# A shared ring of PSUM banks, wide feed-forward norms, and two moved steps in a two-layer fp32 trunk on one core

## The chip, the cores and the metric

The kernel runs on one core of one Trainium2 chip, as one launch. The metric is device time in microseconds (us). Five engines work side by side: PE (TensorE: matmuls and transposes), DVE (VectorE), ACT (ScalarE), POOL (GpSimd) and SP (SyncE, which here only issues transfers). PE writes its products to PSUM, which has eight banks of 128 partitions x 512 fp32 numbers.

## The reference

A trunk of two layers works on 512 tokens of width 1024, in fp32. A layer is: half a feed-forward block, a mixer, a cross-attention to 256 memory tokens, half a second feed-forward block. Every step normalises x and adds its result to x:

```python
for layer in range(2):
    x = x + 0.5 * swiglu(rmsnorm(x, ffn_pre_norm[layer]), w_gu, w_down)      # 1024 -> 2 x 2816 -> 1024
    h = rmsnorm(x, mix_norm[layer])
    x = x + (even_mixer(h) if layer == 0 else mla_mixer(h))
    x = x + memory_cross_attention(rmsnorm(x, ...), rmsnorm(mem, ...))       # 4 heads of 256
    x = x + 0.5 * swiglu(rmsnorm(x, ffn_post_norm[layer]), w_gu, w_down)
```

`rmsnorm(x, g)` is x * rsqrt(mean(x*x) + 1e-6) * g. The mixer of layer 1 (MLA) projects h to a query latent of 512, a key-value latent of 256 and 32 rotary columns, normalises both latents, expands them to 16 heads of 96 (queries and keys) and 64 (values), and does causal softmax attention.

## The kernel before

**Data.** x lies transposed, as eight tiles `x0` to `x7` of 128 features x 512 tokens. Each matmul operand is split into a high part and a low remainder (fp32r), and `mm3` makes one product of three matmuls: high x high, low x high, high x low. Weights come from memory in granules of up to 512 KB (`gran`): SP issues the transfer, ACT casts the high part (L112), POOL, in some places DVE, subtracts to get the low part (L117). The raw tiles have three buffers and the split ones four, so the splitting runs some groups ahead of the matmuls.

**Order.** The program is written for a scheduler that puts instructions on each engine's queue by its own estimate of when they can start; where two could, the earlier one in the program goes first. `with self.queued():` only orders: what is in it goes behind the last recorded matmul on PE. A tile with `bufs=n` gets one of n places as it comes free, and the wait for its last readers is put on the instruction that writes it.

**Norms.** The gain is folded into the operands (`prep`), and the factor 1/rms per token is applied afterwards. `squares` sums the squares of x over the eight tiles into `sqs` (128 x 512). `stats` then sums over the partitions with four one-column products (tokens onto partitions: L172, an fp32 product is two records in the profile), and `rsqrt` works on 128 x 4 numbers by a bit estimate and three Newton steps, 11 DVE instructions in all. In the feed-forward block the factors must stand along the free dimension: four DVE instructions put them on diagonals (`dg`), `spread` multiplies those by ones (L189, four products of 128 columns), and ACT copies the result to `rbc`. `stats` is queued behind group `s0` of the up projection and `spread` behind the next. A group is 24 matmuls of 512 columns. `gated` then multiplies each group by `rbc` on DVE and frees its bank. There are five `mm` banks, two `A` banks and one for the norms (`st`). `s0` is 0, but 3 in the first block, where the first two groups use the `A` banks.

**Launch.** SP issues the first weight granule in two parts (128 KB and 384 KB), then `x1` to `x7`; ACT issues the gains and `x0`. ACT casts part one, makes the high part of `x0` (L150), casts part two, makes the high part of `x1`, and so on. PE meanwhile runs 12 products of a tile of ones with itself (L75).

**MLA.** `mla_in` makes the query latent (`cq`), then the key-value latent token tile by token tile on four banks; after all four it runs `lora` for `cq` and for `ckv`: an `rsqrt`, a scaling on DVE (L642), transposes on PE into two `tp` banks (L646), a cast by ACT (L649) and a subtraction by DVE. In `mla_attn`, one turn of the loop does, in program order: the logits of head n on three `lg` banks (`scores`: matmuls, a maximum on DVE, the exponential on ACT, L871), the transposes of head n-1's exponentials (`weights`: three units on two `pt` banks, L885, copied out by ACT L890 or DVE L892), the transposes of queries and keys of head n+2 (`turn`: one `pt` bank each, L780, read by ACT and DVE), and some projections as filling. One `av` bank and two `A` banks make up the eight.

**Cross-attention.** `memkv` projects the memory in four chunks c of four granules q. After chunk 0 its own norm is finished. `fins` (transposes of a key head into `at`, two banks, L1074, read by ACT L1078 and DVE L1079) are queued behind granules (1, 3), (2, 1), (2, 3) and (3, 1). The `stats` of x for the queries is queued at the end of chunk 1 and uses an `at` bank too.

Of the kernel before, what the change touches and what calls it, by code (L numbers as in the profile page):

```python
# [14 lines left out]
P = 128  # L15
D = 1024
S = 512
KT = D // P
# [3 lines left out]
EPS = 1e-6  # L22
# [4 lines left out]
class Trunk:  # L27
# [32 lines left out]
    def constants(self):  # L60
        nc, cp, a = self.nc, self.cp, self.a
        self.gc = self.t(cp, [P, 10, KT], "gc")
        self.ones = self.t(cp, [P, P], "ones")
        nc.vector.memset(self.ones, 1.0)
        self.x = [self.t(self.xp, [P, S], f"x{f}") for f in range(KT)]

        nc.scalar.dma_start(out=self.gc, in_=a["gcols"])
        nc.scalar.dma_start(out=self.x[0], in_=a["xT"][0])
        self.first = self.first_gran(a["w_gu0"][0]) if self.stop in (None, 1) else None
        for f in range(1, KT):  # L70
            nc.sync.dma_start(out=self.x[f], in_=a["xT"][f])

        ps = self.psA()
        for _ in range(12):
            nc.tensor.matmul(ps[:, 0:P], lhsT=self.ones, rhs=self.ones, start=True, stop=True)  # L75
        self.ident = self.t(cp, [P, P], "ident")
        make_identity(nc, self.ident)
        self.rbc = self.t(cp, [P, S], "rbc")
# [11 lines left out]
    def first_gran(self, src):  # L90

        nc = self.nc
        raw = self.t(self.wr, [P, KT * P], "wr")
        hi = self.t(self.ws, [P, KT * P], "wh", F32R)
        lo = self.t(self.ws, [P, KT * P], "wl", F32R)
        parts = (slice(0, 2 * P), slice(2 * P, KT * P))
        for c in parts:
            nc.sync.dma_start(out=raw[:, c], in_=src[:, c])

        def split(i):  # L100
            self.split(hi[:, parts[i]], lo[:, parts[i]], raw[:, parts[i]])
        r = lambda z: z.rearrange("p (k c) -> p k c", k=KT)
        return r(hi), r(lo), split
# [22 lines left out]

    def rsqrt(self, ssq, n, scale, eps, shape=None):

        nc, sp = self.nc, self.sp
        v = self.t(sp, [P, n], "rs_v", bufs=3)  # L130
        nc.vector.tensor_scalar(out=v, in0=ssq, scalar1=scale, scalar2=eps, op0=ALU.mult, op1=ALU.add)
        y = self.t(sp, [P, n], "rs_y", bufs=3)
        nc.vector.tensor_scalar(out=y.bitcast(I32), in0=v.bitcast(I32), scalar1=-0.5, scalar2=float(0x5F3759DF),
                                op0=ALU.mult, op1=ALU.add)
        u = self.t(sp, [P, n], "rs_u", bufs=2)
        for _ in range(3):
            nc.vector.tensor_tensor(out=u, in0=y, in1=y, op=ALU.mult)
            nc.vector.scalar_tensor_tensor(out=u, in0=u, scalar=-0.5, in1=v, op0=ALU.mult, op1=ALU.mult)
            nc.vector.scalar_tensor_tensor(out=y, in0=u, scalar=1.5, in1=y, op0=ALU.add, op1=ALU.mult)
        return y  # L140

    def prep(self, g, f):

# [23 lines left out]
    def stats(self, pp, tag, bufs=None, bc=False):  # L167

        nc = self.nc
        ps = self.t(pp, [P, S], tag, bufs=bufs)  # L170
        for t in range(NT):
            nc.tensor.matmul(ps[:, t:t + 1], lhsT=self.sqs[:, t * P:(t + 1) * P], rhs=self.ones[:, 0:1],  # L172
                             start=(t == 0), stop=(t == NT - 1), skip_group_check=True)
        y = self.rsqrt(ps[:, 0:NT], NT, 1.0 / D, EPS)
        self.rc = self.t(self.sp, [P, NT], "rc", bufs=2)
        nc.vector.tensor_copy(out=self.rc, in_=y)
        if not bc:
            return
        self.dg = self.t(self.sp, [P, NT, P], "dg", bufs=1)
        for t in range(NT):  # L180
            nc.vector.tensor_scalar(out=self.dg[:, t, :], in0=self.ident, scalar1=self.rc[:, t:t + 1], scalar2=None,
                                    op0=ALU.mult)

    def spread(self, pp, tag, bufs=None):

# [45 lines left out]
    def ffn(self, w_gu, w_dn, g_next, out=None):  # L231
        nc, tc = self.nc, self.tc
        with tc.tile_pool(name=self.nm("ffn"), bufs=1) as fp, \
                tc.tile_pool(name=self.nm("ffps"), bufs=5, space=bass.MemoryType.PSUM) as pp:
            H = NFF // 2


            s0 = 3 if self.first else 0
            todo = []

            def gated(j, pg, pu):
                t1 = self.t(fp, [P, S], "t1", bufs=2)
                t2 = self.t(fp, [P, S], "t2", bufs=2)
                nc.vector.tensor_tensor(out=t1, in0=pg, in1=self.rbc, op=ALU.mult)  # L244
                nc.scalar.activation(out=t1, in_=t1, func=AF.Silu)
                nc.vector.tensor_tensor(out=t2, in0=pu, in1=self.rbc, op=ALU.mult)  # L246
                nc.vector.tensor_tensor(out=t2, in0=t2, in1=t1, op=ALU.mult)  # L247
                ah = self.t(fp, [P, S], f"ah{j}", F32R)
                al = self.t(fp, [P, S], f"al{j}", F32R)
                self.split(ah, al, t2, "act", "dve")  # L250
                return ah, al

            for half in range(2):
                acts = []
                for j in range(H):
                    jj = half * H + j

                    pg, pu = [self.psA() if self.first else self.t(pp, [P, S], "mm") for _ in range(2)]
                    for ps, w in ((pg, w_gu[jj]), (pu, w_gu[NFF + jj])):
                        wh, wl = self.first[:2] if self.first else self.gran(w, KT, P)  # L260
                        self.first = None
                        for k in range(KT):
                            self.mm3(ps, (wh[:, k, :], wl[:, k, :]), (self.hh[k], self.hl[k]), k == 0, k == KT - 1)
                        n = 2 * jj + (ps is pu)
                        if n in (s0, s0 + 1):
                            with self.queued():
                                self.stats(pp, "st", 1, True) if n == s0 else self.spread(pp, "st", 1)
                    todo.append((j, pg, pu))
                    if 2 * jj > s0 or s0 == 0:
                        for z in todo:  # L270
                            acts.append(gated(*z))
                        todo = []
                for m in range(KT):
                    ps = self.psA()
                    for k0, nk in ((0, 6), (6, 5)):
                        wh, wl = self.gran(w_dn[half * KT + m, :, k0 * P:(k0 + nk) * P], nk, P)
                        for k in range(nk):
                            self.mm3(ps, (wh[:, k, :], wl[:, k, :]), acts[k0 + k], k0 + k == 0, k0 + k == H - 1)
                    nc.vector.scalar_tensor_tensor(out=self.x[m], in0=ps, scalar=0.5, in1=self.x[m],  # L279
                                                   op0=ALU.mult, op1=ALU.add)  # L280
                    if half == 1:
                        if g_next is not None:
                            self.prep(g_next, m)
                            self.squares(m)
                        if out is not None:
                            nc.sync.dma_start(out=out[m], in_=self.x[m])
# [366 lines left out]
    def mla_in(self, p, pp, cT, krr, skr, lg, tk):  # L653
        nc, a = self.nc, self.a
        w = a["mla_w_inq"]
        cq = self.t(p, [P, NT, 512], "cq")
# [3 lines left out]
        s1 = self.t(p, [P, NT], "ls1")  # L660
        s2 = self.t(p, [P, NT], "ls2")
        ps = self.banks(pp, "mmmm")
# [6 lines left out]
        ps = self.banks(pp, "AAmm")  # L669
        kv = self.tok_rows(ps, [(a["mla_w_inkv"][:, k0 * 288:(k0 + nk) * 288], nk)  # L670
                                for k0, nk in ((0, 3), (3, 3), (6, 2))], 288, True)
        for t in kv:
# [2 lines left out]
            nc.scalar.activation(out=scr[:, 0:256], in_=ckv[:, t, :], func=AF.Square, accum_out=s2[:, t:t + 1])  # L675
            nc.scalar.activation(out=kr[:, t, :], in_=ps[t]()[:, 256:288], func=AF.Copy, scale=r)
            nc.scalar.activation(out=scr[:, 0:32], in_=kr[:, t, :], func=AF.Square, accum_out=skr[:, t:t + 1])
        self.lora(p, pp, cq, 512, s1, cT, lg, 0)
        self.lora(p, pp, ckv, 256, s2, cT, lg, 4)
        tm = self.t(p, [P, NT, 16], "krt")  # L680
        for o, (x, y, op) in enumerate((("c1", "s2", ALU.subtract), ("s1", "c2", ALU.add))):
# [5 lines left out]
    def mla_attn(self, p, pl, pp, cT, krr, skr, gqk, neg, tq, o):  # L687
# [86 lines left out]
        def turn(st, h):  # L774

            r = []
            for src, nm in ((st["qs"], "q"), (st["ks"], "k")):
                ps = self.t(pp, [P, S], "pt", bufs=2)
                for t in range(NT):
                    self.pe = nc.tensor.transpose(out=ps[0:96, t * P:(t + 1) * P], in_=src[:, t, h, :], identity=self.ident)  # L780
                hi = self.t(p, [96, S], f"{nm}Th", F32R, bufs=3)
# [59 lines left out]
        def scores(n, qk):  # L841
# [6 lines left out]
                self.sums = self.t(p, [P, 2, NT], "asm", bufs=2)  # L848
            sm = self.sums[:, n % 2]
            for u, blks in enumerate(((3,), (2, 0), (1,))):  # L850
                z = self.t(pp, [P, S], "lg", bufs=3)
                for x, i in enumerate(blks):
                    c0 = QA[i][1]
                    wd = (i + 1) * P
# [21 lines left out]
        def weights(pb, wT, units):  # L876

            for u in units:
                blks = ((0,), (1, 3), (2,))[u]
                ps = self.t(pp, [P, S], "pt", bufs=2)  # L880
                for j in blks:
                    c0 = KA[j][1]
                    for i in range(j, NT):
# [117 lines left out]
    def memkv(self, p, pp, l, kT, V, gqk):  # L1001
# [24 lines left out]
        for c in range(4):  # L1026
# [12 lines left out]
            if rm is None:  # L1039
# [4 lines left out]
                y = self.rsqrt(st[:, 0:MT], MT, 1.0 / D, EPS)  # L1044
                rm = self.t(p, [P, MT], "rm")
                nc.vector.tensor_copy(out=rm, in_=y)
            if c == 1:

                with self.queued():
                    self.stats(pp, "at", 2)  # L1050
# [208 lines left out]
```

## Time and profile before

| | |
|---|---|
| median of three runs | 2269.89 us (2269.11 to 2270.17) |
| the profiled execution | 2276.53 us |
| its span, first to last instruction | 2274.8 us |
| PE busy in the span | 2248.7 us (99%) |
| DVE, ACT, POOL busy | 893.8, 865.5, 1017.5 us |

The profile describes one execution. Its span is 1.7 us below that execution's own time, and that time is 6.6 us over the median of the runs. A line of the timeline reads: start, duration, engine, line of the kernel, operation, tile written and tiles read, shape, count, and in brackets how long the engine stood idle before it and which instruction ended that.

### The profile page before, as it was taken

What the parts mean: (1) busy time and instruction counts of PE and PEld (TensorE: products, weight loads), DVE (VectorE), ACT (ScalarE), POOL (GpSimd) and SP (SyncE); (2) the same over time, 40 slices, a digit from 0 to 9 for tenths busy, and PEclk for the clock granted to TensorE, in tenths of its full rate; (3) what the DMA queues carried; (4) which work ended last, traced back from release to release, by engine and by line L of the source; (5) the groups of instructions that cost most, each with busy time, mean ns of one, the idle gap of its engine ahead of it and who ended that gap; (6) DMA issues with size and microseconds to landing.
All of it is one profiled execution on the core that took longest, in us unless ns stands there. A gap on an engine that the chain in (4) does not pass through costs nothing. (4 is left out here: it accounts for less than half of the span.)

```text
span 2274.8 us, 27672 instructions
## 1 busy us (share of the span) xinstructions
PE 2248.7 (99%) x10496; PEld 1851.0 (81%) x10496; DVE 893.8 (39%) x1697; ACT 865.5 (38%) x1428; POOL 1017.5 (45%) x854
## 2 busy tenths in 40 slices
PE   9999999999999999999999999999999999999999
PEld 7888888777888888888888888887777788888887
DVE  5211223465745422123422022377667555221220
ACT  5222233456544322223322222356656443222221
POOL 5545546112143454555554555536321424545543
PEclk9999999999999999999999999999999999999999
DMA  5223323211432322332322332321113312323222
GB/s 167 87 85 116 93 84 130 84 54 54 139 107 66 93 93 84 111 93 82 113 93 83 113 96 85 99 86 56 38 37 122 121 56 93 93 83 113 93 83 94
DMA packets 67493, 208.60 MB, mean 92 GB/s; under 512 B 8608, under 2 KB 10784, under 8 KB 67360
## 3 DMA queue, kind: packets, MB, share of 16 engines
q1 hardware_dynamic: 67072, 206.52, 29.4%
q8 instruction: 83, 1.36, 0.2%
q14 instruction: 50, 0.41, 0.1%
q10 hardware_dynamic: 288, 0.30, 0.1%
HBM read 204.70 MB, written 2.10 MB: 91 GB/s over the span
## 5 line engine op out<-in xcount | busy, mean ns | idle before, releaser
L117 POOL TENSOR_TENSOR wl<-wr,wh 128x512 fp32r<-128x512 f32 (+2 forms) x752 | 941.7, 1273 | 1048.5 <-ACT wh L112 1048.1
L112 ACT CAST wh<-wr 128x1024 fp32r<-128x1024 f32 (+2 forms) x422 | 406.7, 964 | 1059.7 <-PE mm L124 573.5
L123 PE MATMUL mm<-hh,wh 128*128 128x512 f32 x1408 | 548.7, 390 | 0.0
L125 PE MATMUL mm<-hh,wl 128*128 128x512 f32 x1408 | 547.9, 389 | 0.0
L124 PE MATMUL mm<-hl,wh 128*128 128x512 f32 x1408 | 547.8, 389 | 0.0
L124 PEld LDWEIGHTS mm<-hl,wh 128*128 128x128 f32 x1408 | 264.3, 188 | 55.1
L123 PEld LDWEIGHTS mm<-hh,wh 128*128 128x128 f32 x1408 | 264.3, 188 | 54.8
L125 PEld LDWEIGHTS mm<-hh,wl 128*128 128x128 f32 x1408 | 264.3, 188 | 54.7
L123 PE MATMUL A<-ah,wh 128*128 128x512 f32 x704 | 277.4, 394 | 0.0
L125 PE MATMUL A<-ah,wl 128*128 128x512 f32 x704 | 276.0, 392 | 0.0
L124 PE MATMUL A<-al,wh 128*128 128x512 f32 x704 | 273.2, 388 | 0.0
L246 DVE TENSOR_TENSOR t<-mm,rbc 128x512 f32<-128x512 f32 x87 | 60.2, 692 | 389.3 <-PE mm L125 389.3
L279 DVE SCALAR_TENSOR_TENSOR x<-A,x 128x512 f32<-128x512 f32 x64 | 44.3, 692 | 357.7 <-PE A L125 357.7
L125 PEld LDWEIGHTS A<-ah,wl 128*128 128x128 f32 x704 | 132.1, 188 | 31.0
L124 PEld LDWEIGHTS A<-al,wh 128*128 128x128 f32 x704 | 132.1, 188 | 29.6
L123 PEld LDWEIGHTS A<-ah,wh 128*128 128x128 f32 x704 | 132.4, 188 | 26.4
L244 DVE TENSOR_TENSOR t<-mm,rbc 128x512 f32<-128x512 f32 x87 | 60.2, 692 | 190.6 <-PE mm L125 185.3
L88 DVE TENSOR_TENSOR al<-t,ah 128x512 fp32r<-128x512 f32 x88 | 84.3, 958 | 58.4 <-ACT ah L84 58.4
L123 PE MATMUL A<-hh,wh 128*128 128x512 f32 x256 | 103.8, 405 | 1.4 <-ACT hh L150 1.2
L124 PE MATMUL A<-hl,wh 128*128 128x512 f32 x256 | 101.2, 395 | 0.8 <-DVE hl L151 0.8
L125 PE MATMUL A<-hh,wl 128*128 128x512 f32 x256 | 101.1, 395 | 0.6 <-POOL wl L117 0.6
L84 ACT CAST ah<-t 128x512 fp32r<-128x512 f32 x88 | 54.6, 621 | 64.9 <-DVE t L247 64.7
(348 smaller groups left out, 2991.9 us busy)
## 6 DMA issues: line engine op xcount, KB each, us to landing
wr<-in_w_gu SPq DMA_DIRECT2D x175, 512.0 KB, 3.5
wr<-in_w_dn SPq DMA_DIRECT2D x64, 384.0 KB, 3.1
wr<-in_w_dn SPq DMA_DIRECT2D x64, 320.0 KB, 2.9
wr<-in_xmem_wkv SPq DMA_DIRECT2D x32, 512.0 KB, 3.7
wr<-in_xmem_wq SPq DMA_DIRECT2D x16, 512.0 KB, 3.5
wr<-in_xmem_wo SPq DMA_DIRECT2D x16, 512.0 KB, 3.6
wr<-in_sbg_w_zv SPq DMA_DIRECT2D x12, 512.0 KB, 3.6
wr<-in_sbg_w_qk SPq DMA_DIRECT2D x8, 512.0 KB, 3.6
```

What stands on the lines that cost most here:

```text
L84: nc.scalar.copy(out=hi, in_=src)
L88: e.tensor_tensor(out=lo, in0=src, in1=hi.bitcast(F32), op=ALU.subtract)
L112: nc.scalar.copy(out=hi, in_=raw)
L117: e.tensor_tensor(out=lo_[:, c], in0=raw[:, c], in1=hi[:, c].bitcast(F32), op=ALU.subtract)
L123: mm(out, lhsT=A[0], rhs=B[0], start=start, stop=False, skip_group_check=True)
L124: mm(out, lhsT=A[0], rhs=B[1], start=False, stop=False, skip_group_check=True)
L125: self.pe = mm(out, lhsT=A[1], rhs=B[0], start=False, stop=stop, skip_group_check=True)
L244: nc.vector.tensor_tensor(out=t1, in0=pg, in1=self.rbc, op=ALU.mult)
L246: nc.vector.tensor_tensor(out=t2, in0=pu, in1=self.rbc, op=ALU.mult)
L279: nc.vector.scalar_tensor_tensor(out=self.x[m], in0=ps, scalar=0.5, in1=self.x[m], op0=ALU.mult, op1=ALU.add)
```

## The change

1. **Launch.** SP issues the first part of the granule, `x0`, `x1`, the second part, then `x2` to `x7`; ACT issues only the gains. PE runs 7 products of ones, not 12.
2. **Feed-forward norms.** `stats_rows` replaces `stats` and `spread` in `ffn`: one product of ones (128 x 128) with `sqs` (128 x 512) puts every token's sum on all partitions, and the `rsqrt` runs on 128 x 512 numbers and ends in `rbc`. Its two helper tiles come from the pool of `sq`.
3. **Latents.** `lora` for `cq` stands behind token tile 1 of the key-value latent, no longer behind tile 3.
4. **Ring.** The three `lg` and two `pt` banks become five banks with one tag, `z`.
5. **Moved sums.** The `stats` of x in `memkv` moves from the end of chunk 1 to the end of chunk 2.

```diff
         nc.scalar.dma_start(out=self.gc, in_=a["gcols"])
-        nc.scalar.dma_start(out=self.x[0], in_=a["xT"][0])
         self.first = self.first_gran(a["w_gu0"][0]) if self.stop in (None, 1) else None
-        for f in range(1, KT):
+        for f in range(2 if self.first else 0, KT):
             nc.sync.dma_start(out=self.x[f], in_=a["xT"][f])
-        for _ in range(12):
+        for _ in range(7):
             nc.tensor.matmul(ps[:, 0:P], lhsT=self.ones, rhs=self.ones, start=True, stop=True)
...
-        for c in parts:
-            nc.sync.dma_start(out=raw[:, c], in_=src[:, c])
+        nc.sync.dma_start(out=raw[:, parts[0]], in_=src[:, parts[0]])
+        for f in range(2):
+            nc.sync.dma_start(out=self.x[f], in_=self.a["xT"][f])
+        nc.sync.dma_start(out=raw[:, parts[1]], in_=src[:, parts[1]])
...
+    def stats_rows(self, pp, tag, bufs=None):
+        nc = self.nc
+        ps = self.t(pp, [P, S], tag, bufs=bufs)
+        self.pe = nc.tensor.matmul(ps, lhsT=self.ones, rhs=self.sqs, start=True, stop=True)
+        v = self.t(self.sp, [P, S], "sq", bufs=2)
+        u = self.t(self.sp, [P, S], "sq", bufs=2)
+        self.rsqrt_into(self.rbc, v, u, ps, 1.0 / D, EPS)
...
-                        if n in (s0, s0 + 1):
+                        if n == s0:
                             with self.queued():
-                                self.stats(pp, "st", 1, True) if n == s0 else self.spread(pp, "st", 1)
+                                self.stats_rows(pp, "st", 1)
...
-        self.lora(p, pp, cq, 512, s1, cT, lg, 0)
+            if t == 1:
+                with self.queued():
+                    self.lora(p, pp, cq, 512, s1, cT, lg, 0)
         self.lora(p, pp, ckv, 256, s2, cT, lg, 4)
...
-                ps = self.t(pp, [P, S], "pt", bufs=2)
+                ps = self.t(pp, [P, S], "z", bufs=5)
                 for t in range(NT):
...
-                z = self.t(pp, [P, S], "lg", bufs=3)
+                z = self.t(pp, [P, S], "z", bufs=5)
                 for x, i in enumerate(blks):
...
-                ps = self.t(pp, [P, S], "pt", bufs=2)
+                ps = self.t(pp, [P, S], "z", bufs=5)
                 for j in blks:
...
-            if c == 1:
+            if c == 2:
                 with self.queued():
                     self.stats(pp, "at", 2)
```

`rsqrt_into` is the old body of `rsqrt` with the tiles handed in; the places that call `rsqrt` do as before.

## Rows read from the trace of the kernel before

**Rows 1.** The head of the profile page: the span, then each engine's busy us, its share and its instructions.

```profile
span 2274.8 us, 27672 instructions
PE 2248.7 (99%) x10496; PEld 1851.0 (81%) x10496; DVE 893.8 (39%) x1697; ACT 865.5 (38%) x1428; POOL 1017.5 (45%) x854
```

**Rows 2.** The waits of PE over the whole span: what waited, for what, us in total, times, longest.

```profile
PE pt L780 <- DVE wT L892: 4.2, 6, 1.4
PE A L123 <- ACT sq L758: 2.5, 1, 2.5
PE at L172 <- DVE kl L1079: 2.1, 2, 1.7
...
PE A L123 <- ACT ch L649: 1.4, 1, 1.4
...
PE pt L780 <- DVE qTl L88: 1.2, 1, 1.2
PE pt L780 <- DVE sqr L736: 1.1, 1, 1.1
PE pt L780 <- ACT wT L890: 1.0, 4, 0.3
```

**Rows 3.** [...]

```profile
1612.60:1615.80 3.20, 3.20 (x12) 3.20 (x11) 1.29 (x2) 0.68 (x1) 3.20 (x7) 0.50 0.00 0
1766.20:1769.40 3.20, 3.20 (x9) 2.51 (x8) 3.20 (x20) 1.04 (x1) 0.00 (x0) 0.50 0.19 28
1769.80:1773.00 3.20, 3.20 (x17) 2.64 (x16) 1.30 (x3) 1.78 (x3) 0.00 (x0) 1.00 0.72 245
...
1.10:4.80 3.70, 3.68 (x17) 3.68 (x18) 0.43 (x1) 1.69 (x2) 0.28 (x1) 1.00 0.75 198
```

**Rows 4.** The timeline of the launch, PE, ACT and DVE.

```profile
1.12 4.70 PE L75 MATMUL A<-ones 128*128 128x128 f32 x24 [1.12 <-DVE ones L64]
...
6.23 0.72 ACT L150 ACTIVATE hh<-x,gc 128x512 fp32r<-128x512 f32 x1 [2.29 <-DMA x<-in_xT]
...
7.00 0.50 PE L123 MATMUL A<-hh,wh 128*128 128x512 f32 x1 [1.18 <-ACT hh L150]
...
8.58 4.72 DVE L151 SCALAR_TENSOR_TENSOR hl<-x,gc,hh 128x512 fp32r<-128x512 f32 x7
...
15.90 0.50 PE L125 MATMUL A<-hh,wl 128*128 128x512 f32 x1 [0.63 <-POOL wl L117]
```

**Rows 5.** Transfers: issuing queue, count, KB of one, us from issue to landing.

```profile
x<-in_xT ACTq DMA_DIRECT2D x1, 256.0 KB, 4.9
...
wr<-in_w_gu SPq DMA_DIRECT2D x1, 128.0 KB, 2.7
```

**Rows 6.** The timeline at the start of layer 0's second feed-forward block, PE, DVE and POOL.

```profile
765.36 0.95 PE L172 MATMUL st<-ones,sqs 128*128 128x1 f32 x8
766.17 0.49 PE L123 MATMUL mm<-hh,wh 128*128 128x512 f32 x1
...
771.76 1.05 PE L189 MATMUL st<-dg,ones 128*128 128x128 f32 x8
772.56 0.48 PE L123 MATMUL mm<-hh,wh 128*128 128x512 f32 x1
...
762.82 1.77 DVE L165 TENSOR_TENSOR sqs<-sqs,sq 128x512 f32<-128x512 f32 x1
...
775.41 0.69 DVE L247 TENSOR_TENSOR t<-t,t 128x512 f32<-128x512 f32 x1 [0.66 <-ACT t L245]
...
772.89 2.55 POOL L117 TENSOR_TENSOR wl<-wr,wh 128x512 fp32r<-128x512 f32 x2 [3.84 <-ACT wh L112]
```

**Rows 7.** The timeline of the MLA latents, PE, ACT and DVE.

```profile
1519.73 1.04 PE L646 MATMUL tp<-ident,cq 128*128 128x128 f32 x8
1522.13 0.45 PE L123 MATMUL A<-wh,ch 128*128 128x384 f32 x1 [1.36 <-ACT ch L649]
...
1521.39 0.69 ACT L649 ACTIVATE ch<-tp,lorag 128x512 fp32r<-128x512 f32 x1
...
1518.27 1.68 DVE L642 TENSOR_SCALAR cq<-cq,rs_y 128x512 f32<-128x512 f32 x4
```

**Rows 8.** The timeline of one turn of the attention loop (logits of head 5), PE, ACT and DVE.

```profile
1610.15 0.64 PE L780 MATMUL pt<-ident,qs 128*96 128x128 f32 x4 [0.90 <-DVE wT L892]
1612.14 0.77 PE L780 MATMUL pt<-ident,ks 128*96 128x128 f32 x4 [1.35 <-DVE wT L892]
...
1609.57 0.36 ACT L871 ACTIVATE pb<-lg,anm 128x128 f32<-128x128 f32 x1
...
1609.91 0.47 ACT L871 ACTIVATE pb<-lg,anm 128x256 f32<-128x256 f32 x1
...
1611.67 0.41 DVE L892 COPY wT<-pt 128x256 f32<-128x256 f32 x1
```

**Rows 9.** The timeline of layer 1's memory projection, PE and DVE.

```profile
1764.02 1.05 PE L172 MATMUL at<-ones,sqs 128*128 128x1 f32 x8 [1.74 <-DVE kl L1079]
...
1763.48 0.48 DVE L1079 SCALAR_TENSOR_TENSOR kl<-at,gqk,kh 128x256 fp32r<-128x256 f32 x1
...
1777.02 0.60 PE L1074 MATMUL at<-ident,tk 128*128 128x128 f32 x4
...
1778.12 0.88 DVE L1079 SCALAR_TENSOR_TENSOR kl<-at,gqk,kh 128x256 fp32r<-128x256 f32 x2
```

More of the change, by code (lines that the diff above doesn't have):

```diff
@@ L127, in rsqrt, with rsqrt_into @@
     def rsqrt(self, ssq, n, scale, eps, shape=None):
-        nc, sp = self.nc, self.sp
+        sp = self.sp
         v = self.t(sp, [P, n], "rs_v", bufs=3)
+        y = self.t(sp, [P, n], "rs_y", bufs=3)
+        u = self.t(sp, [P, n], "rs_u", bufs=2)
+        self.rsqrt_into(y, v, u, ssq, scale, eps)
+        return y
+    def rsqrt_into(self, y, v, u, ssq, scale, eps):
+        nc = self.nc
         nc.vector.tensor_scalar(out=v, in0=ssq, scalar1=scale, scalar2=eps, op0=ALU.mult, op1=ALU.add)
-        y = self.t(sp, [P, n], "rs_y", bufs=3)
         nc.vector.tensor_scalar(out=y.bitcast(I32), in0=v.bitcast(I32), scalar1=-0.5, scalar2=float(0x5F3759DF),
                                 op0=ALU.mult, op1=ALU.add)
-        u = self.t(sp, [P, n], "rs_u", bufs=2)
         for _ in range(3):
@@ L139, in rsqrt @@
             nc.vector.scalar_tensor_tensor(out=y, in0=u, scalar=1.5, in1=y, op0=ALU.add, op1=ALU.mult)
-        return y
     def prep(self, g, f):
@@ L182, in stats @@
                                     op0=ALU.mult)
+    def stats_rows(self, pp, tag, bufs=None):
+        nc = self.nc
+        ps = self.t(pp, [P, S], tag, bufs=bufs)
[3 more added lines that the diff above has]
+        self.rsqrt_into(self.rbc, v, u, ps, 1.0 / D, EPS)
     def spread(self, pp, tag, bufs=None):
```

## The prediction

> **What bounds the kernel now.** The head of the page comes first: PE is busy 2248.7 of 2274.8 us [rows 1], the other engines under half. PE is the bound, and a change can help in three ways only: PE does less work, PE stands still less (26.1 us in all), or PE runs less of its work at the low clock. Second, PE's list of waits [rows 2], which names the places. A few lines carry it: the attention of layer 1 waits 7.5 us in the four lines on `pt` (4.2 + 1.2 + 1.1 + 1.0), the memory projection 2.1 us in its `stats`, the latents 1.4 us on a cast. The 2.5 us on L758 is an activation's square, which this change does not touch. Third, the granted clock by stretches [rows 3]: in two of those shown, right behind long waits, the clock is at 0.50. In the one at 1766 PE has 9 matmuls in 3.2 us, in the next 17. Last, the timelines of the five edited places [rows 4 to 9].
>
> **Feed-forward norms, four blocks.** The removed pieces are seen start to start: the one-column products take PE from 765.36 to 766.17, 0.81 us, the spreading from 771.76 to 772.56, 0.80 us [rows 6]. The new product passes the same 512 columns through the same kind of fp32 product as the spreading did, so I take its 0.80 us. The 0.81 us goes. One change between kinds of product goes too; it has no row of its own and can't cost more than the 0.49 us of the record behind it, of which I put in a tenth. Taken 0.85 a block, **3.4 us**; bounds 2.8 (the wide product is 0.15 slower) to 4.0.
>
> On DVE the eleven instructions of the chain go from 128 x 4 to 128 x 512 numbers. The nearest rows of that size are 0.69 us for a product of two tiles and 1.77 us for a sum of two tiles that ran beside POOL [rows 6], so the chain takes 7.6 to 19.5 us. It is costed at nothing, because the banks cover it. Sums end at 766.2, so `rbc` is there between 773.8 and 785.7. Group 0's bank is next wanted by group 5. A group takes 5.6 us (766.17 to 771.76), groups 2 to 4 begin about 772, so group 5 begins about 788.5. Even the slow chain and one multiplication, 786.4, comes before. In the first block the sums stand behind group 3 and group 7 wants group 2's bank, again three groups or 16.8 us later, but two groups are multiplied first: at 19.5 + 2 us that is 4.7 us late, once. POOL works 2.55 of 5.6 us, so I expect some 10 us and nothing lost. Behind the chain on DVE stand only the gate's own instructions. ACT loses its copy.
>
> POOL, in turn, may be held up by the chain. Its split at 772.89 goes into the buffer that the group just ended has freed, so it is wanted four groups later, about 789. It ends at 775.4; even 7.6 us more leaves 5 us. [...]
>
> **Ring, 16 heads.** A turn of the loop asks for banks in the order logits L0 L1 L2, transposes P0 P1 P2, query Q, key K. Before, the last five share two banks, so K waits until DVE has copied P2, and Q until P0 or P1 is copied. With five in a ring, P2 takes L0's bank, Q that of L1, K that of L2, each freed by an exponential. In the turn shown [rows 8], K starts at 1612.14, behind a copy begun at 1611.67. L2's exponential is over at 1610.38. L1's is over at 1609.93, so Q gains little (1610.15 to about 1610.0), and K can follow at 1610.4 to 1610.6. Of 2.25 us of waiting some 1.6 go, 70%. Of 7.5 us that is 5.3; I take **5.0 us**, with bounds 3.0 (only K gains) and 9.5 (all, with 0.15 us of refilling saved at each of 13 waits). The ring adds a wait too: the next L1 and L2 must wait for the copies of P1 and P2, and all of PE is queued behind. But a filling of twelve matmuls comes first, over 2 us, and the last copy ends 0.06 us before K's start even now.
>
> The low clock at 1612.6 [rows 3] follows 2.25 us of waiting with four transposes between. PE's work in it would take half: 1.6 us. If the waits shrink to 0.7 us I expect no drop; taken **1.2 us**, bounds 0 and 1.6.
>
> **Moved sums, two layers.** The 2.1 us [rows 2] arise because an `at` bank comes free only when DVE, busy with two chains, has made the key's low part at 1763.48 [rows 9]. At the new place the transposes run at 1777.02 and both low parts are made from 1778.12 to 1779.00, so the sums meet a free bank after about 1.6 us, which the matmuls put between fill or nearly fill. Taken **1.9 us**, bounds 1.2 and 2.4 (with refilling). The result is first wanted after chunk 3, 48 matmuls or 11 us later (a group's 24 take 5.6 us, 0.233 each): its 4-column chain is hidden. The low clock at 1766.2 goes with the 1.74 us wait: 8 of 17 matmuls are missing from 3.2 us, 1.5 us; taken **1.2 us**, bounds 0 and 1.5.
>
> **Latents.** The scaling ends at 1519.95, the transposes start at 1519.73, and ACT casts only at 1521.39, after other work; PE waits 1.36 us [rows 7]. Ahead of tile 3's work ACT could cast at about 1520.6, which is 0.8 us. Against it: if the transposes are queued among tile 3's matmuls, PE stands at them until the scaling is done, and 24 matmuls stand behind. Those matmuls then cover the cast, so the loss is at most about 1.5 us. Taken **0.5 us**, bounds -1.5 and 1.4.
>
> **Launch.** ACT's first use of `x0` is at 6.23, PE's first matmul at 7.00 [rows 4]; the transfer took 4.9 us, the 128 KB before it 2.7 us [rows 5]. Directly behind those, 256 KB at the 198 GB/s of this stretch [rows 3] is 1.3 us: `x0` lands near 4.8, 1.3 us earlier. SP issues one transfer more ahead of `x2`, ACT one fewer; bytes ahead of `x2` are the same, and from there DVE's 0.67 us a tile (4.72 / 7) sets the pace. Part two comes later than now, and on ACT `x1` may stand behind its cast. Taken **1.2 us**. Upper bound 2.0, with the 0.63 us wait at 15.90. Lower bound -2.4: 24 records of ones take 4.70 us, so 14 end near 4.0, and the clock may not have risen by then; 18 of the first group's matmuls, 4.2 us, would then take 17/9 of that [rows 3], 3.7 us more, less the 1.3 us.
>
> **Sum.** 3.4 + 5.0 + 1.2 + 1.9 + 1.2 + 0.5 + 1.2 = 14.4 us. The profiled execution took 2276.5 us (span 2274.8 and 1.7 around it) and would take 2262.1. It is 6.6 us over the median of the runs; taken off 2269.9, the forecast is **2255.5 us**.
>
> **Rivals.** (A) The exponentials are as late as the copies. For: Q in the row shown gains 0.15 us only. Against: K's 1.7. Half the ring's gain and its clock stretch go, 3.7 us: 2259.2. (B) The clock rises late in the launch, because PE stops its products of ones before it is granted. For: the idle second that follows. Against: 2.7 of the 4.7 us of products remain. 3.6 us go, to the lower bound: 2259.1. [...] (C) PE is early but what it needs is not: in attention it then waits for the norms and low parts that DVE makes, and ring, its clock stretch and latents bring nothing, 6.7 us: 2262.2. For: the L736 line, a norm's factor. Against: it is 1.1 of 7.5 us. (D) The other side: the wide chain holds the feed-forward banks. At the longest row, 1.77 us for each instruction, that is the 4.7 us in the first block: 2260.2. To end 0.2% slower than before it must cost 18.9 us, 4.7 a block: `rbc` at about 792.5, 26 us for eleven instructions, 2.4 us each, which no row comes near. (E) The scheduler, with other tiles to place, moves waits elsewhere and the total stays: about 2269.9.
>
> **Chances.** Forecast 0.50, A 0.18, B 0.13, C 0.10, D 0.06 (0.02 of it on the slower side), E 0.03. The bounds add up to 2247.4 at best and 2266.8 at worst; ends rarely meet, so 8 in 10 is 2249 to 2263, which takes in A, B, C and the small D. Within 0.2% (4.5 us, about what a measurement of this kernel can tell from no change) lie E and C's tail: 0.05. Slower 0.02, faster 0.93.
>
> **What would show it.** Feed-forward: no L189 in those blocks, one product of about 0.8 us, the first multiplication by `rbc` 8 to 12 us after it, no wait of PE on `mm` banks. Ring: the lines on `wT` and `qTl` nearly gone, shorter waits on `pb`. Memory: no wait at `stats`, no 0.50 stretch behind it. Latents: L649 right behind the transposes. Launch: first matmul near 5.6. I am wrong if PE waits on the multiplication by `rbc`, if new waits in attention sum to over 3 us, or if the clock is low in the first group.

## The result, and the profile after

The changed kernel takes 2254.17 us (median of 4 runs, 2254.0 to 2254.84) against 2270.03 us for the kernel before in the same comparison: a ratio of 0.9928, 95% interval 0.9911 to 0.9945, so 15.9 us faster. The forecast was 2255.5 us, 1.3 us too long. Its terms fit less well than its sum: the ring with its clock stretch was 4 us too small, and three others were too large.

The head of the page of after, and PE's waits over the whole span (what waited, for what, us in total, times, longest). The waits are to be laid beside [rows 2].

```profile
span 2252.3 us, 27515 instructions
PE 2234.0 (99%) x10430; PEld 1838.2 (82%) x10430; DVE 928.9 (41%) x1677; ACT 860.1 (38%) x1424; POOL 1021.7 (45%) x854
```

```profile
PE A L124 <- ACT sq L776: 2.5, 1, 2.5
...
PE z L798 <- DVE wT L910: 1.2, 2, 0.7
...
PE tp L661 <- issue: 0.7, 1, 0.7
...
PE at L177 <- DVE kl L1097: 0.4, 1, 0.4
...
```

The 7.5 us on `pt` have become 1.2 us on `z` (L798 is the old L780), and the wait at `stats` 0.4 us. L661 are the transposes of the latents (the old L646). The 2.5 us behind the query's square is where it was; the change does not touch it.

The two profiled executions differ by 22.5 us of span, the medians by 15.9. The table sets the starts of the same work against each other (us from the start of the first instruction named to that of the last, from the timelines; the first row counts from the start of the span). It includes one kernel with only the ring and one with only the new norms, both from the experiments below.

| stretch | before | ring alone | norms alone | after |
|---|---|---|---|---|
| launch and first feed-forward block | 372.30 | 371.86 | 371.47 | 371.73 |
| mixer of layer 0, scores to memory projection | 131.77 | 128.61 | 128.64 | 128.67 |
| memory projection, layer 0 | 48.31 | 48.43 | 48.33 | 47.89 |
| second feed-forward block, layer 0 | 181.99 | 182.03 | 181.06 | 181.04 |
| latents to their first expansion | 15.23 | 15.22 | 15.23 | 14.64 |
| attention, first turn to last values | 162.38 | 151.93 | 162.47 | 151.71 |
| memory projection, layer 1 | 51.57 | 48.91 | 48.51 | 48.35 |

Two rows fall by about 3 us in all three other kernels, changed or not there: the mixer of layer 0 and layer 1's memory projection. Those 6 us were a property of the one profiled execution of before, which was 6.6 us over its median. In the mixer the cause is a stretch at the low clock, seen here for before (the columns, here and in [rows 3]: from:to, length, busy us and instructions of PE, PEld, DVE, ACT and POOL, TensorE's granted clock as a share of the full one, transfer share, GB/s):

```profile
472.47:479.30 6.83, 6.83 (x18) 5.20 (x19) 3.73 (x10) 4.79 (x10) 0.00 (x0) 0.50 0.14 55
479.30:486.10 6.80, 6.80 (x39) 5.98 (x39) 3.17 (x5) 2.81 (x5) 0.00 (x0) 1.00 0.13 31
```

### The profile page after: what moved, and what is told of

It is laid out like the page before. It is cut to its first block, busy times and chain, and to the rows that moved or that the text cites. A ratio compares the mean times of both kernels' runs of the same rounds, so it can differ in the third digit from the quotient of the medians.

```text
span 2252.3 us, 27515 instructions
## 1 busy us (share of the span) xinstructions
PE 2234.0 (99%) x10430; PEld 1838.2 (82%) x10430; DVE 928.9 (41%) x1677; ACT 860.1 (38%) x1424; POOL 1021.7 (45%) x854
```

## The experiments

Theory 1 reads the terms from the two traces and leaves out low-clock stretches that only the one execution had. Theory 2 is the forecast's own terms. Medians of kernels in one comparison share its runs of before.

**Each part alone, on the kernel before.** The edits are the hunks of the diff above: the three lines of `turn`, `scores` and `weights`; `rsqrt_into`, `stats_rows` and the line in `ffn`; the one line of the memory projection; the two places of `lora`.

> The kernel before with the ring of five banks alone. Theory 1 (terms read from the two traces, with the low-clock stretches left out because only the profiled execution of before had them): from the first turn to the last values the span is 10.7 us shorter, one stretch of 3.4 us at half clock lies in it (1.7 us), so the ring is worth 9.0 us and the time is about 2261.0. Theory 2 (the terms of the forecast, clock stretch included in the ordinary runs): 5.0 + 1.2 = 6.2 us, about 2263.8. Rival (the exponentials are as late as the copies): 2.5 us, about 2267.5.

> The kernel before with the wide product in the four feed-forward blocks alone. Theory 1: 0.95 us in each of three blocks by the traces and 0.85 in the first, 3.7 us, time about 2266.3. Theory 2 (forecast): 3.4 us, about 2266.6. [...]

> The kernel before with the sums of the memory projection behind chunk 2 instead of chunk 1, alone. Theory 1 (no low clock in ordinary runs): 1.5 us in layer 1 and 0.4 in layer 0, 1.9 us, time about 2268.1. Theory 2 (the low-clock stretch belongs to ordinary runs too): 1.9 + 1.2 = 3.1 us, about 2266.9.

> The kernel before with the transposes of the query latents issued behind tile 1's statistics alone. Theory 1: the start of the transposes to the first expansion is 0.6 us shorter by the traces, time about 2269.4. Theory 2 (forecast): 0.5 us, 2269.5. Rival (the transposes hold up tile 3's matmuls): up to 1.5 us slower, 2271.5.

| alone | median, us | against before (2269.87) | ratio, 95% interval |
|---|---|---|---|
| ring | 2259.70 | -10.2 | 0.9955 [0.9943, 0.9968] |
| norms | 2266.61 | -3.3 | 0.9983 [0.9974, 0.9992] |
| moved sums | 2268.39 | -1.5 | 0.9997 [0.9988, 1.0006] |
| latents | 2269.23 | -0.6 | 0.9999 [0.9990, 1.0008] |

The ring is worth far more than the forecast's 6.2 us: its interval goes from 7.3 to 12.9 us and takes in theory 1's 9.0. The norms agree with both theories, and 4.7 us lost in the first block, rival D of the prediction, are excluded. The moved sums and the latents can't be told from nothing by their intervals; the traces do it below. The four differences add up to 15.6 of the 15.9 us. Each is known to some 2 us only, so this shows no more than that the parts neither help nor hinder each other by much.

Where the ring's gain lies, as PE's waits from the first turn to the last values: the norms alone (the old banks), then the ring alone.

```profile
PE pt L794 <- DVE wT L906: 4.2, 6, 1.4
PE pt L794 <- DVE sqr L750: 1.1, 1, 1.1
PE pt L794 <- ACT wT L904: 1.0, 4, 0.3
PE pt L794 <- POOL wl L117: 1.0, 1, 1.0
PE av L926 <- DVE arT L921: 0.6, 1, 0.6
PE pt L899 <- ACT wT L904: 0.4, 1, 0.4
```

```profile
PE z L780 <- DVE wT L892: 1.2, 2, 0.7
PE av L912 <- DVE arT L907: 0.6, 1, 0.6
```

Some 8.3 us of waits become 1.8. And the clock: the norms alone once more (old banks), a stretch of the attention, and the same place with the ring alone.

```profile
1607.09:1610.51 3.42, 3.42 (x13) 3.42 (x12) 0.98 (x2) 0.60 (x1) 3.42 (x7) 0.50 0.00 0
1610.51:1613.93 3.42, 3.42 (x27) 3.28 (x26) 2.32 (x6) 2.07 (x5) 0.99 (x2) 1.00 0.00 0
```

```profile
1607.90:1611.30 3.40, 3.40 (x26) 3.34 (x25) 1.84 (x5) 2.75 (x10) 2.47 (x4) 1.00 0.02 5
```

All five traced kernels with the old banks have this stretch, and none of the nine with a new sharing of them: this one belongs to ordinary executions. With 13 records in place of 27 it costs half of 3.42 us, 1.7 us. Waits 6.5 and clock 1.7 leave some 2.3 of the 10.5 us. Most of that is what the list does not name at each wait: in before's trace the transposes on `pt` (L780) start 0.11 us apart and take 0.27 each, and the list counts a wait from the end of the record ahead, so it costs some 0.16 us more than listed. For the eleven waits that the ring removes this makes 1.8 us, an estimate from these numbers.

Which banks the ring gives out is seen in the turn of [rows 8] with the ring alone (PE, then ACT, then DVE):

```profile
1602.13 0.60 PE L780 MATMUL z<-ident,qs 128*96 128x128 f32 x4
1603.19 0.64 PE L780 MATMUL z<-ident,ks 128*96 128x128 f32 x4 [0.46 <-DVE wT L892]
...
1601.15 0.58 ACT L890 COPY wT<-z 128x512 f32<-128x512 f32 x1
...
1602.04 0.58 ACT L871 ACTIVATE pb<-z,anm 128x384 f32<-128x384 f32 x1 [0.31 <-DVE anm L867]
...
1602.95 0.47 ACT L871 ACTIVATE pb<-z,anm 128x256 f32<-128x256 f32 x1
...
1602.46 0.68 DVE L892 COPY wT<-z 128x512 f32<-128x512 f32 x1
```

The prediction gave Q the bank of L1 and K that of L2. But Q starts at 1602.13, with no wait, while the exponential of L1 (the row of 384 columns) is still reading, and K at 1603.19, before that of L2 (256 columns) ends at 1603.42. The places are given out as they come free, not in turn: only L0's bank (its exponential ended at 1601.16) and P0's (copied by ACT until 1601.73) were free when P2 and Q started, so these two have them, and K waited until DVE had copied P1, at 1603.14. Here the exponentials of L1 and L2 are as late as the copies, as rival A had it, and Q's wait is gone all the same.

**Which of the ring's requests was late.** Here the key draws from the logits' banks and everything else stays as it was:

```diff
-                ps = self.t(pp, [P, S], "pt", bufs=2)
+                ps = self.t(pp, [P, S], *(("pt", F32, 2) if nm == "q" else ("lg", F32, 3)))
```

> The kernel before, where the key's transposes alone draw from the three banks of the logits; the query's stay in the two banks of the weights' transposes. The forecast's step (K can go ahead, Q gains little, 70% of the waits are K's): the larger part of the ring's 10.2 us, about 7, time about 2262.9. Other reading (Q waits as long as K does, for the copy of the second transposed bank): about half, 5 us, 2264.9. If the exponentials are as late as the copies: 2 us or less, 2268.

Measured: 2265.29 us against 2270.28, 5.0 us less (ratio 0.9983 [0.9974, 0.9992]). The other reading holds: the interval, 1.8 to 5.9 us, leaves out the 7, and the key is about half of the ring's gain. PE's waits from the first turn to the last values:

```profile
PE pt L780 <- ACT wT L890: 1.5, 5, 0.5
PE pt L780 <- DVE sqr L736: 1.1, 1, 1.1
PE pt L780 <- DVE wT L892: 0.9, 1, 0.9
...
```

3.5 us of waits on `pt` at L780 remain, and with the key elsewhere they are all the query's. The ring leaves 1.2 us on that line. By the traces the key alone takes 5.5 us off the attention (156.89 against 162.38, the low clock included), and the ring 5.0 us more. So the query had about as much to gain as the key. The trace of before shows this already when its 16 turns are added up: PE stands 4.1 us ahead of the query's transposes and 3.3 us ahead of the key's.

**The launch.** First the launch's hunks alone on the kernel before (transfers and 7 products of ones).

> The kernel before with the launch's transfers in the new order and 7 products of ones, alone. Theory 1 (the first groups are bound by tiles and casts on ACT and DVE, not by the first matmul or the clock): the first matmul comes 1.4 to 1.9 us earlier and the start of the second group does not; gain 0.0, at most 0.5 either way, time about 2269.9. Theory 2 (forecast): 1.2 us, 2268.7. Rival B of the forecast (the clock rises late): 2.4 us slower, 2272.3.

Measured: 2270.04 us against 2270.28, ratio 1.0001 [0.9992, 1.0010]. Nothing, as theory 1 had it; the interval alone, 1.8 us faster to 2.3 slower, would leave room for the forecast's 1.2, the trace does not. It shows why neither the early start nor the clock counts. PE (start, duration, line, tile written and read; a line may stand for several):

```profile
4.96 0.79 PE L124 MATMUL A<-hh,wh 128*128 128x512 f32 x1 [0.48 <-ACT hh L151]
...
7.19 0.63 PE L125 MATMUL A<-hl,wh 128*128 128x512 f32 x1
7.62 0.63 PE L126 MATMUL A<-hh,wl 128*128 128x512 f32 x1
8.55 0.79 PE L124 MATMUL A<-hh,wh 128*128 128x512 f32 x1 [0.31 <-ACT hh L151]
9.58 0.50 PE L125 MATMUL A<-hl,wh 128*128 128x512 f32 x1 [0.24 <-DVE hl L152]
9.92 0.40 PE L126 MATMUL A<-hh,wl 128*128 128x512 f32 x1
10.16 0.39 PE L124 MATMUL A<-hh,wh 128*128 128x512 f32 x1
```

The matmuls run 0.43 us apart up to 7.6 and 0.24 us apart from 9.9: half pace at first (read off the matmuls: the clock column has no lower grant there). Yet PE still waits for tiles at 8.55 and 9.58. What sets the pace from the second group on is POOL, which makes the low parts of the weights one after another. The kernel with the ring alone (old launch), then the launch alone:

```profile
14.14 12.28 POOL L117 TENSOR_TENSOR wl<-wr,wh 128x512 fp32r<-128x512 f32 x8 [12.76 <-ACT wh L112]
```

```profile
14.68 14.58 POOL L118 TENSOR_TENSOR wl<-wr,wh 128x512 fp32r<-128x512 f32 x10 [13.30 <-ACT wh L113]
```

POOL starts when ACT has cast the second group's weights. With the new launch that is 0.5 us later in this pair, although PE's first matmul is 1.6 us earlier (4.96 against 6.58). Executions differ here, but the new launch is never clearly earlier: POOL starts between 13.9 and 14.6 us in the six traces with the old launch and between 14.2 and 14.7 in the four with the new one (all with the squares where they were). The whole first block ends at 372.65 in the trace of the launch alone, against 371.66 to 372.30 in the five with the old launch and the old norms, so it is no shorter there, and rather longer. In both launches ACT does squares of the norm ahead of that cast: three of the eight with the old one, four with the new one. The last two stand right before it, here in the trace of after:

```profile
12.54 1.14 ACT L169 ACTIVATE sq<-x 128x512 f32<-128x512 f32 x2
13.59 1.03 ACT L113 CAST wh<-wr 128x1024 fp32r<-128x1024 f32 x1
```

So the squares were moved, on the changed kernel, behind the cast of the third group:

```diff
-        nc.scalar.copy(out=hi, in_=raw)
+        self.cast = nc.scalar.copy(out=hi, in_=raw)
...
+                        if s0 and n == 2:
+                            with self.tc.issue_after(self.cast.ins):
+                                for f in range(KT):
+                                    self.squares(f)
...
-        for f in range(KT):
-            self.squares(f)
```

> The changed kernel, where the eight squares of the launch are issued on ACT behind the weight cast of the third group. Theory (the second group waits for its cast, which stands behind five squares on ACT): the second group begins about 1.0 us earlier and the low part of its weights too; 1.0 us faster than the changed kernel, 2253.2. Rival (the launch is bound by its transfers, or the time is given back at the sums after the fourth group): same, 2254.2.

Measured: 2252.55 us (ratio to before 0.9926 [0.9914, 0.9939]). The interval overlaps that of the changed kernel; the trace is clearer. The cast begins at 12.03 and POOL at 13.16, 1.5 us earlier; the third group begins 1.8 us earlier, and no block after it gives any of that back. The cast now waits 0.56 us for the transfer of its weights, so behind the squares the transfer is the next limit.

```profile
12.03 1.05 ACT L113 CAST wh<-wr 128x1024 fp32r<-128x1024 f32 x1 [0.56 <-DMA wr<-in_w_gu]
```

Two variants of this kernel ask what the clock and the transfers are then worth: one with 10 products of ones in place of 7, and one with the launch of before.

> As after_squares, with 10 products of ones in place of 7, so that PE works until its first tile is there. In after_squares the first nine matmuls ran at half pace until 8.95 us. Theory 1 (tiles and casts set the end of the first group anyway): 0.0 to 0.5 faster than after_squares. Theory 2 (with the squares out of the way the late clock is what is left): 1.0 to 1.8 us faster than after_squares, about 2251.2.

> As after_squares, but with the launch's transfers and 12 products as in the kernel before. Theory 1 (the new order of transfers is worth the 1.2 us of the forecast once the squares are behind the casts, and lost it to them in the changed kernel): 1.2 us slower than after_squares, 2253.8. Theory 2 (the transfers are worth nothing either way, the squares all of it): same as after_squares, 2252.6.

Measured: 2253.77 us (2252.65 to 2256.27) and 2253.56 us (2252.52 to 2254.46). Ten products bring nothing: in their trace the third group begins 0.2 us later than with seven. With the old launch it begins at 19.57 us against 19.59, and the first block ends at 369.89 against 369.91. So the new order of transfers is worth nothing with or without the squares in the way; the second theory of that run holds. The 1 us between the medians is no more than the runs spread. With the old launch the trace puts 1.0 us into layer 1's memory projection, far from the launch; with ten products it has two low-clock stretches, also far from it, that the trace with seven lacks.

**How much the banks cover.** The changed kernel with `range(6)` for `range(3)` in the wide chain alone:

> The changed kernel with six steps of the wide rsqrt chain in place of three: nine more instructions on DVE, by the trace of after some 9.1 us, so the chain takes 20.3 us and not 11.2. Theory (the banks cover about 20 us in three blocks; in the first, whose product stands behind group 3, the cover ends 3.3 us behind the chain of now): 5.8 us late, once, time about 2260.0. Rival (the chain holds banks in every block when it is this long): 5 us and more in each, 2270 and above. If DVE's backlog costs nothing anywhere: 2254.2.

Measured: 2262.89 us (2260.66 to 2267.31), 8.7 us more than the changed kernel's median. By the traces 8.5 of the 9.0 us between the two spans come in the first block; the other three are as long as in after. The first block's wait, and the clock behind it:

```profile
PE mm L124 <- DVE t L259: 5.4, 1, 5.4
```

```profile
54.26:61.08 6.82, 5.97 (x14) 4.75 (x15) 6.82 (x9) 3.64 (x7) 2.97 (x2) 0.50 0.09 14
61.08:67.90 6.82, 6.82 (x31) 5.61 (x31) 5.69 (x7) 2.60 (x4) 3.27 (x2) 1.00 0.17 66
```

The 5.8 us expected are there as 5.4 of waiting. What no theory had is the half clock behind it, 6.82 us long, another 3 us. So the cover of the wide chain is real, and its edge lies where the forecast put it: only in the first block.

**The 2.5 us behind the query's square.** ACT's square waits for a buffer that DVE frees late, because DVE multiplies three heads' key norms first. Two attempts: those of heads 1 and 2 behind the next sums (on the changed kernel), and three buffers for squares in place of two (on the one with the squares late).

```diff
-                for h in range(3):
-                    normed(h)
+                normed(0)
...
+            if g == 1 and t in (1, 2):
+                normed(t)
```

> The changed kernel, where the key norms of heads 1 and 2 of the first group of heads are multiplied on DVE behind the next group's query sums of tiles 1 and 2, and not ahead of them. Theory: the 2.5 us wait of PE behind the query squares comes from ACT's squares, which wait for a sq buffer that DVE frees only after six multiplications; it goes, but the norm of head 1 then ends about 1 us later than the first transposes want it: 1.5 us faster than the changed kernel, 2252.7, and 1.7 us more in executions that have the low clock behind this wait. Rival (the wait moves to the key's transposes in full): same, 2254.2.

> As after_squares, with three buffers for the squares in place of two, so that ACT's query squares of tile 2 need not wait for DVE's sum of tile 0's successor behind six multiplications. Theory: the 2.5 us wait of PE behind the query squares shrinks to under 1 us; 1.0 to 2.0 us faster than after_squares, about 2251. Rival (the wait moves on to the next square or to the key's transposes, as in after_reduce): same, 2252.6.

Measured: 2255.22 us (2254.15 to 2255.73) and 2252.38 us (2250.93 to 2253.45). Both rivals hold. The first transposes start 2.7 and 2.8 us earlier than those of the kernel each was made from, counted from the expansion, but at the logits of the first head PE then waits for the high part of the key (`kTh`), 3.0 and 2.2 us in place of 0.3.

```profile
PE z L124 <- ACT kTh L806: 3.0, 1, 3.0
```

```profile
PE z L124 <- ACT kTh L809: 2.2, 1, 2.2
```

Counted from the expansion, the first logits start as late as without the edit in the first attempt and 0.9 us earlier in the second, and both traces have a low-clock stretch behind that. Neither helps by its median. The squares' order is the one edit here that does: 1.8 us by the third group in the traces, 1.6 us between the medians, which their intervals do not tell apart.

## Why the prediction was right, and where not

**Base.** The forecast took its microseconds off the median, but read them in an execution 6.6 us over it. It should have asked which of them that excess already held. The low clock at 1766 was one: of six traced kernels with the sums at the old place two have it (before, and the key from the logits), of eight with the moved sums none. The term of 1.2 us does not belong to the median.

**Ring, 5.0 us and 1.2 for its clock.** Measured together 10.2. The clock's 1.2 was 1.7. The failed step is "Q gains little", which was read from one turn, [rows 8], and made into 70% for all the waits (13 by the prediction, 12 in the four lines of [rows 2]). It rests on a second one: that P2, Q and K take the banks of L0, L1 and L2 in turn, each freed by an exponential. In that very turn Q had a bank sooner, and K waited for a copy all the same. With the key alone served, half the gain stayed away; the whole removed 84% of the 7.5 us (1.2 left), and the refilling delays of 2 us, which stood in the upper bound alone, came too. By the traces the gain without the clock is 8.8 us, near that bound of 9.5. The prices of rivals A and C are excluded: the lists name no wait on an exponential, and there are 2.1 us of waits in the whole attention of after. A's condition held in the turn shown, though, and it was the order of handing out banks, not an early exponential, that kept it from costing.

**Norms, 3.4 us.** Measured 3.3; by the table 0.95 in a block. The new product and the first matmul behind it take from 761.55 to 762.64, 1.09 us; less the 0.23 us of a matmul that is 0.86, for 0.80 expected. Counted the same way, up to the second matmul behind, the removed pieces of [rows 6] were 0.91 and 0.89 us, so 0.94 goes in a block. PE in layer 0's second block:

```profile
761.55 1.02 PE L194 MATMUL st<-sqs,ones 128*128 128x512 f32 x2
...
762.64 0.40 PE L125 MATMUL mm<-hl,wh 128*128 128x512 f32 x1
```

The chain took 11.1 us, for some 10 expected, and hid as forecast. The last nine of its instructions on DVE in the same block, then POOL beside them:

```profile
764.30 1.66 DVE L143 TENSOR_TENSOR sq<-rbc 128x512 f32<-128x512 f32 x1
765.99 0.69 DVE L144 SCALAR_TENSOR_TENSOR sq<-sq,sq 128x512 f32<-128x512 f32 x1
766.72 0.69 DVE L145 SCALAR_TENSOR_TENSOR rbc<-sq,rbc 128x512 f32<-128x512 f32 x1
767.45 0.69 DVE L143 TENSOR_TENSOR sq<-rbc 128x512 f32<-128x512 f32 x1
768.17 0.69 DVE L144 SCALAR_TENSOR_TENSOR sq<-sq,sq 128x512 f32<-128x512 f32 x1
768.90 0.69 DVE L145 SCALAR_TENSOR_TENSOR rbc<-sq,rbc 128x512 f32<-128x512 f32 x1
769.63 1.66 DVE L143 TENSOR_TENSOR sq<-rbc 128x512 f32<-128x512 f32 x1
771.32 1.66 DVE L144 SCALAR_TENSOR_TENSOR sq<-sq,sq 128x512 f32<-128x512 f32 x1
773.02 0.69 DVE L145 SCALAR_TENSOR_TENSOR rbc<-sq,rbc 128x512 f32<-128x512 f32 x1
```

```profile
762.69 2.72 POOL L118 TENSOR_TENSOR wl<-wr,wh 128x512 fp32r<-128x512 f32 x2 [2.46 <-ACT wh L113]
769.05 3.39 POOL L118 TENSOR_TENSOR wl<-wr,wh 128x512 fp32r<-128x512 f32 x2 [3.64 <-ACT wh L113]
```

The three instructions of 1.66 us begin while POOL works. Of the six of 0.69 us five lie outside its work; the sixth, at 768.90, began 0.15 us before POOL's next pair, and that pair took 3.39 us where the one in [rows 6] took 2.55, so there it was POOL's pair that took longer. The first block shows the same: 1.66 or 1.67 us for the three that begin while POOL works (at 35.12, 40.45 and 42.15), and 3.39 us for POOL's pair at 39.87, which began 0.15 us behind one of 0.69. So the long end of the forecast's range, 19.5 us with all eleven as long as the row beside POOL, was far off: POOL works in 6.1 of the 11.1 us, and three on DVE pay, about 1 us each.

**Moved sums, 1.9 us.** Too large. The wait at the old place differs from execution to execution: 1.7 us in layer 1 in the trace of before, 1.0 in the ring's, 0.8 in the latents', 0.5 in the norms'; the forecast took the largest of these. And at the new place 0.4 to 0.8 us of it stays in layer 1 in four of the eight traced kernels, where a low part of the key is again the last to come (0.4 in the list of after); in the other four nothing does. By the table and the kernel with the sums alone (47.88 and 48.50 us for the two projections) the gain is some 0.4 us in each layer, under 1 us in all, plus a low-clock stretch in one execution of three.

**Latents, 0.5 us.** Measured 0.6 between the medians, within the noise, and 0.6 by the traces (15.23 to 14.64). The objection that the prediction raised came true in part: PE waits 0.7 us at the transposes, among tile 3's matmuls, in place of 1.4 at the cast.

**Launch, 1.2 us.** Measured 0.0. The first matmul came at 5.15, ahead of the 5.6 forecast. The failed step is that from `x2` on "DVE's 0.67 us a tile (4.72 / 7) sets the pace". POOL sets it from the second group on, started by a cast on ACT that stands behind squares in either order of transfers. Rival B was right that the clock can rise late, half pace up to 7.6 us in the trace of the launch alone, and wrong about its price. In after itself the matmuls had full pace from the first (0.23 us apart at 6.28), but in four of the six traced kernels with 7 products the first group ran at half pace, up to 13.4 us, and by the third group that cost nothing. Before's own launch begins at half pace as well, on the products of ones, although the clock column of [rows 3] has 1.00 there: their records (L75) start 0.21 us apart from 1.50 to 4.70 and 0.11 apart from 4.88. After's 14 (L74) all start 0.21 apart from 1.50.

So the sum stood by luck: the ring's missing 4 us made up for the launch, the moved sums and the clock at 1766, some 3.5 us together. The mechanisms of the norms and the latents were right, and so were that of the moved sums, too large as it was taken, and the ring's in the main (transposes no longer wait for copies on two banks), but not its order of banks. Those of the launch and of the second low clock were not.

Not settled is the low clock behind the 2.5 us wait. Six of the seven traced kernels without the whole change have it at about 1548, and four of the seven that have at least its ring, norms, sums and latents; in two of these four it comes behind the wait for the key that took the place of the 2.5 us. After is one of those without: from the matmul behind that wait to the first transposes it takes 1.50 us where before takes 2.73. Whether the change makes it rarer these executions can't tell.

## What to carry to other kernels

When two sets of banks with different holders are used in a fixed order, ask of every request which release it waits for in each arrangement, and read that from all turns of the loop rather than from one. Ask too whether the places go round in a fixed order or as they come free. Before a stall or a slow stretch in a profile is counted as gain, set that execution's time against the median: what only the one execution had can't be won. In a launch, find the engine that sets the pace of the second and third group; an earlier first matmul is no gain while another engine's chain starts no sooner.

## What was not expected of the hardware

TensorE's granted clock was 0.50 in places of a kernel in which PE is 99% busy, mostly behind waits of 1.1 to 5.4 us. Behind the longest it was granted 0.50 for 6.82 us, and 14 matmuls were recorded in place of 31. At about 1610, with the old banks, it came in five of five traced executions; at 1766, with the sums at the old place, in two of six; in the mixer of layer 0, where nothing differs and where before's trace has no wait over 0.2 us in the 17 us ahead of it, in two of fourteen; what brought it there stays open. So a wait's price here is its own length in some executions, and in others more by some 1.2 us (at about 1548), 1.7 (at 1610) or 3 (behind the 5.4 us). And a launch that begins at half pace cost nothing by its third group here: in the trace of the key norms moved behind the sums the first group ran at half pace up to 13.4 us, and the third group began at 20.98 us; in after, at full pace from the first matmul, it began at 21.41.
